# xbc and z of a hybrid encoder layer in one stated order, xbc by half slabs

## The chip, the core and the metric

The kernel runs on one core of a Trainium2 chip. The metric is the device time of one execution in microseconds. Three executions of the kernel before took 1104.84, 1105.65 and 1106.17 us (median 1105.65). The engines are named as in the profile: PE (TensorE), ACT (ScalarE), DVE (VectorE), POOL (GpSimd), SP (SyncE, which here only issues DMAs).

## The reference

One encoder layer on 256 tokens of width 2048, in float32. The part that matters here is the first of three blocks:

```python
hn = rmsnorm(h, mix_norm_pre[i])
proj = hn @ w_in[i]
z, xbc, dt_raw, u = jnp.split(proj, split_at, axis=-1)
y_ssd = ssd_mixer(z, xbc, dt_raw, ssd_conv_w[i], ssd_conv_b[i], ssd_dt_bias[i],
                  ssd_a_log[i], ssd_d[i], ssd_norm[i])
y_pool = pool_mixer(u, pool_w[i], pool_scale[i])
mix = jnp.concatenate([y_ssd, y_pool], axis=-1) @ w_out[i]
h = h + rmsnorm(mix, mix_norm_post[i])
```

and inside the mixer (`y` is a scan over the tokens in both directions, in chunks of 128):

```python
xbc = jax.nn.silu(dwconv_centred(xbc, conv_w, conv_b))
xs, bm, cm = jnp.split(xbc, [D_SSD, D_SSD + G * SSD_STATE], axis=-1)
...
y = y_fwd + y_bwd + xs.astype(F32) * d_skip.astype(F32).reshape(G, E)[:, :, None]
y = y.reshape(b, L, D_SSD) * jax.nn.silu(z.astype(F32))
y = y.reshape(b, L, G, D_SSD // G)
y = y * lax.rsqrt(jnp.mean(y * y, axis=-1, keepdims=True) + EPS)
```

z has 1024 columns, xbc 1536 (xs 1024, B 256, C 256). Behind this block come a gated MLP (up and down, width 5632) and a per-layer embedding, which the change does not touch.

## The kernel before

Every float32 product is made of three matmuls. Each operand is split into a high part (ACT's cast, L157, or `put`) and a low part (DVE's subtraction, L158), and high x high, high x low and low x high are summed in PSUM (`mm`, L90). `split` makes the two halves of one weight piece of 128 x 1024 in one of five weight buffers; the weights come over SP into one of three raw buffers. Names in the profile end in `w` for such a pair (`wo010_0w`: output projection, half 0, rows from 10 x 128, piece 0).

The stages follow one another on PE: dtu to 52 us, xbc 52 to 141, z 141 to 196, the output projection (`wo`, two halves of 1024 columns) 196 to 284, then up, down and the embedding.

**xbc** has three slabs of 512 columns, computed as columns x tokens: `feature_major` (L371) loads the weights of a slab in four pieces of two k-pairs and issues for each k and each 128 columns three matmuls of 256 tokens, summed in one PSUM tile. Behind each slab `times_rows` (L451), `conv` (L459, five taps: one on ACT, four on DVE), tanh on ACT and a last DVE product make the convolved, activated slab `cv`. Slab 2 holds B and C, slabs 0 and 1 hold xs.

**Jobs.** Between the pieces of xbc and z, `aside` (L220) pops a list of jobs from `work` and runs them: `pool_mix` (mx) and `pool_map` (pw) of the pooling mixer, `decays` (dps), `seg_sums` (cps, seg_x, seg_w), `seg` (eight segment-sum tiles, into E), `cb` (products of C and B), `weigh` (E times dt and cb), `xs_turn` (transposes, xt), `far`, `skip` and `mix` (four parts of y: matmuls yo and yd, additions on DVE). The jobs `early_fetch` and `early_add` prepare block sums of w_out for the units (0,0), (0,2), (1,0) and (1,2) of the output projection: fetch 1 MB, four additions of 512 columns in place (L275, `add_blocks`), store to DRAM over POOL's queue.

**z** (`token_major`, L330) is computed as tokens x columns in four PSUM tiles, z0_0 to z1_1. Behind it y is gated with silu(z) (tanh L812 on ACT, L813 and L814 on DVE), squared and summed (L815, ACT), the scale computed on POOL (L410 to L817), y scaled (L820, DVE) and transposed by PE (yt, L827) as the left operand of the projection. The projection begins with the rows of the pooling mixer (wo08 to wo014), which do not need y.

**Seven products.** Some units of the projection (wo00, wo02, wo112, wo10, wo12) are made with seven block products in place of eight (`seven_products`, L277): aw and bw are splits of the weights, dw and cw of their block sums. If the sums were prepared, they are loaded (tile `t`); otherwise DVE makes them in place between bw and dw.

**What sets the order.** A tile scheduler orders each engine's instructions, and assigns buffers, from the program's order and its own estimates. `in_order()` (L205) chains the instructions of ACT, DVE and SP that a block issues, so that they keep the order of the code; before, xbc and z are not in such a block. `load` issues DMAs on SP. PSUM has six main tiles and two misc tiles.

Of the kernel before, what the change touches and what calls it, by code (L numbers as in the profile page):

```python
# [17 lines left out]
P = 128  # L18
L = 256
# [34 lines left out]
def build(nc, a, out):  # L54
# [6 lines left out]
    with tile.TileContext(nc) as tc, \  # L61
# [208 lines left out]
        def add_blocks(r, t=None):  # L270
# [3 lines left out]
            for i, a, b in ((1, v, 0), (0, v, 3), (3, s, 1), (2, s, 3)):  # L274
                nc.vector.tensor_add(s[:, i], v[:, i], a[:, b])  # L275

# [94 lines left out]
        def feature_major(name, w, get, acc):  # L371

            for u in range(4):
                r = raw(f"{name}r{u}", w[u])
                for j in range(2):
                    wh, wl = split(f"{name}{u}_{j}", r[:, j * 1024:(j + 1) * 1024], 1024)
                    for kk in range(2):
                        k = 4 * u + 2 * j + kk
                        xh, xl = get(k)
                        for f in range(4):  # L380
                            s = slice(kk * 512 + f * P, kk * 512 + (f + 1) * P)
                            for q, (ww, xx) in enumerate(((wh, xh), (wh, xl), (wl, xh))):
                                mm(acc[f // 2][:, f % 2 * L:(f % 2 + 1) * L], ww[:, s], xx,
                                   k == 0 and q == 0 and f % 2 == 0, k == NK - 1 and q == 2)
                aside()

# [64 lines left out]
        def times_rows(name, acc, rb):  # L451
            o = mid(name)
            for i in range(2):
                nc.vector.tensor_tensor(o[:, i * 512:(i + 1) * 512].rearrange("p (f t) -> p f t", f=2),
                                        acc[i].rearrange("p (f t) -> p f t", f=2),
                                        rb.unsqueeze(1).to_broadcast([P, 2, L]), op=ALU.mult)
            return o

        def conv(name, acc, taps, wcol, wstep, bcol):  # L459

            cv = mid(name)
            half = taps // 2
            for f in range(4):
                o, i = cv[:, f * L:(f + 1) * L], acc[:, f * L:(f + 1) * L]
                nc.scalar.activation(o, i, AF.Identity, bias=vec(bcol + f), scale=vec(wcol + half * wstep + f))
                for j in range(taps):
                    d = j - half
                    if d == 0:
                        continue
                    lo, hi = max(0, -d), L - max(0, d)  # L470
                    nc.vector.scalar_tensor_tensor(o[:, lo:hi], i[:, lo + d:hi + d], vec(wcol + j * wstep + f),
                                                   o[:, lo:hi], op0=ALU.mult, op1=ALU.add)
            return cv


        hn = Panel("hn")
# [136 lines left out]
        ee = [page(f"E{t}") for t in range(2)]  # L613

        def seg_sums():

            cps = misc("cps")
            for a_ in range(4):
                mm(cps[:64, a_ * P:(a_ + 1) * P], da4[:, a_ // 2, a_ % 2].rearrange("p r h -> p (r h)"),
                   mask[:, 3 * (a_ % 2), :], True, True)  # L620
            hi, c = page("seg_h", F32R)[:64, :512], page("seg_c")[:64, :512]
            nc.scalar.copy(hi, cps[:64, :])
            nc.vector.scalar_tensor_tensor(c, hi.bitcast(F32), low, cps[:64, :], op0=ALU.mult, op1=ALU.add)
            c4 = c.rearrange("p (a l) -> p a l", a=4)
            for i in range(4):
                nc.scalar.activation(seg_x[:32, :, i, :], c4[:32], AF.Copy, scale=among[:32, i:i + 1])
            for i in range(4):
                nc.scalar.activation(seg_w[32:64, :, i, :], c4[32:], AF.Copy, scale=four[32:, i:i + 1])

        def seg(i):  # L630
            t, q = divmod(i, 4)
            ps = [misc(f"seg{i}{d}") for d in range(2)]
            for d in range(2):
                mm(ps[d], seg_w[:, 2 * t + d, q], seg_x[:, 2 * t + d].rearrange("p i l -> p (i l)"), True, True)
            e = ee[t][:, q * 512:(q + 1) * 512]
            nc.scalar.copy(e, ps[0])
            nc.vector.tensor_tensor(e, ps[1], e, op=ALU.min)
            nc.scalar.activation(e, e, AF.Exp)
# [3 lines left out]
        cat.hi, cat.lo = [None, page("cath1", F32R)], [None, page("catl1", F32R)]  # L642
        mixh, mixl = page("mixh", F32R), page("mixl", F32R)
        pw = {}

        def pool_mix(g):
            ps = misc(f"mx{g}")
# [706 lines left out]
```

## Time and profile before

| what | us |
|---|---|
| median of three runs | 1105.65 (1104.84 to 1106.17) |
| the profiled execution's own time | 1104.97 |
| its span | 1103.2 |
| PE busy | 1096.7 |
| DVE busy | 977.2 |
| ACT busy | 729.1 |
| xbc, first matmul | 52.24 |
| z, first matmul | 140.67 |
| output projection, first matmul | 196.31 |

The granted clock of PE was 0.999 over the span. Times of the trace count from the span's start. A row of the page's groups of instructions gives line, engine, operation, output and input, count, then busy time, mean ns of one, and the idle time before them with what ended it. A row of the timeline gives start, length, engine and line; in brackets stands how long the engine stood idle before it and who ended that. A row of the chain of waits gives start, length and what ran.

### The profile page before, as it was taken

The numbers are of one execution on the slowest core, as the hardware profiler recorded it, in microseconds if no ns is written. First come the engines' busy times: TensorE is split into PE (matmuls) and PEld (weight loads), VectorE is DVE, ScalarE is ACT, GpSimd is POOL, SyncE is SP. The second block draws the span as 40 slices with busy tenths as digits, with TensorE's granted clock in tenths as the row PEclk, the third lists the DMA queues.
The fourth block names the chain that finished last, engine by engine and source line by source line (L and its number), as shares of the span: only waits on it lengthen the run. The fifth ranks groups of instructions, "written<-read, shape, count | busy, mean of one in ns | idle before, by whom it ended". The sixth has DMA issues, their size and how long they took to land.

```text
span 1103.2 us, 16052 instructions
## 1 busy us (share of the span) xinstructions
PE 1096.7 (99%) x5961; PEld 948.8 (86%) x5961; DVE 977.2 (89%) x1373; ACT 729.1 (66%) x1068; POOL 84.9 (8%) x145
## 2 busy tenths in 40 slices
PE   9999999999999999999999999999999999999998
PEld 9999988888888888888888888888888888888886
DVE  6589998898868998889889988898999999999997
ACT  6858763566776565655656646657688878786773
POOL 0200000100100000000000000000000000051001
PEclk9999999999999999999999999999999999999999
DMA  9895259556489999989999998999999989996872
GB/s 363 359 339 195 101 183 367 209 195 244 158 367 388 408 397 364 403 344 367 383 366 383 364 391 345 404 362 420 367 410 375 378 335 389 419 379 224 317 276 77
DMA packets 57247, 361.71 MB, mean 328 GB/s; under 512 B 6352, under 2 KB 7504, under 8 KB 21200
## 3 DMA queue, kind: packets, MB, share of 16 engines
q1 hardware_dynamic: 45648, 298.71, 69.0%
q0 software_dynamic: 11088, 61.35, 14.5%
q8 instruction: 47, 0.77, 0.3%
q10 hardware_dynamic: 432, 0.62, 0.2%
q14 instruction: 32, 0.26, 0.1%
HBM read 306.65 MB, written 54.00 MB: 327 GB/s over the span
## 4 chain that ended last, share of the span: by engine, by line
PE 97%; ACT 1%; DVE 1%; issue 0%; POOL 0%; POOLq 0%; DVEq 0%
PE ga L90 22%; PE va L90 22%; PE dna L90 11%; PE woa L90 7%; PE xbc L90 5%; PE gt L90 5%; PE dns L90 4%; PE dtu L90 4%; PE z L90 4%; PE dn0s L90 2%; PE dn1s L90 2%; PE ple L90 1%; PE gts L90 1%; PE wos L90 1%; PE yd L90 1%; PE pw L90 1%
## 5 line engine op out<-in xcount | busy, mean ns | idle before, releaser
L90 PE MATMUL ga<-wox,ug_0w 128*128 128x512 f32 x704 | 130.8, 337 | 0.0
L90 PE MATMUL ga<-wox,ug_1w 128*128 128x512 f32 x704 | 130.2, 337 | 0.0
L90 PE MATMUL va<-wox,uv_0w 128*128 128x512 f32 x704 | 129.2, 337 | 0.0
L90 PE MATMUL va<-wox,uv_1w 128*128 128x512 f32 x704 | 129.2, 337 | 0.0
L90 PEld LDWEIGHTS ga<-wox,ug_0w 128*128 128x128 f32 x704 | 107.7, 188 | 14.6 <-ACT pl L919 0.2
L90 PEld LDWEIGHTS ga<-wox,ug_1w 128*128 128x128 f32 x704 | 107.5, 188 | 14.5 <-DVE wox L195 0.2
L90 PEld LDWEIGHTS va<-wox,uv_1w 128*128 128x128 f32 x704 | 107.5, 188 | 14.5
L90 PEld LDWEIGHTS va<-wox,uv_0w 128*128 128x128 f32 x704 | 107.5, 188 | 14.5
L275 DVE TENSOR_TENSOR dnb<-dnb 128x512 f32<-128x512 f32 x128 | 88.3, 690 | 3.0
L250 POOL DMA_DIRECT2D dns<-dnb x30 | 16.1, 536 | 319.4 <-DVE dnb L275 279.1
L90 PE MATMUL xbc<-hnh,xb_0w 128*128 128x256 f32 x192 | 37.9, 284 | 0.3 <-ACT u L571 0.3
L90 PE MATMUL xbc<-hnh,xb_1w 128*128 128x256 f32 x192 | 37.1, 283 | 0.0
L846 ACT CAST he<-he 128x512 fp32r<-128x512 f32 x13 | 8.1, 621 | 42.6 <-DVE he L845 42.6
L988 ACT CAST hs<-hid 128x384 fp32r<-128x384 f32 (+1 forms) x44 | 23.4, 537 | 13.7 <-PE dna L90 13.5
L90 PEld LDWEIGHTS xbc<-hnh,xb_0w 128*128 128x128 f32 x192 | 30.8, 189 | 0.9 <-ACT u L571 0.4
L90 PEld LDWEIGHTS xbc<-hnh,xb_1w 128*128 128x128 f32 x192 | 30.7, 189 | 0.1
L1068 ACT ACTIVATE fc<-gr,vt 128x256 f32<-128x256 f32 x44 | 26.1, 593 | 6.9 <-DVE gr L1061 6.9
L90 PE MATMUL dna<-dn_0w,hs 128*128 128x512 f32 x108 | 28.6, 394 | 0.0
L90 PE MATMUL dna<-dn_1w,hs 128*128 128x512 f32 x108 | 28.3, 392 | 0.0
L1139 POOL DMA_DIRECT2D hd<-hsum x24 | 12.9, 539 | 193.1 <-PE dn0s L90 70.4
L989 DVE TENSOR_TENSOR hs<-hid,hs 128x384 fp32r<-128x384 f32 (+1 forms) x44 | 25.4, 581 | 2.6 <-ACT hs L988 2.6
L90 PE MATMUL xbc<-hnl,xb_1w 128*128 128x256 f32 x96 | 27.3, 284 | 0.0
(1781 smaller groups left out, 2871.4 us busy)
## 6 DMA issues: line engine op xcount, KB each, us to landing
dnb<-w_down SPq DMA_DIRECT2D x32, 1024.0 KB, 10.0
dns<-dnb POOLq DMA_DIRECT2D x30, 1024.0 KB, 6.5
hd<-hsum POOLq DMA_DIRECT2D x24, 512.0 KB, 8.2
zr<-w_z SPq DMA_DIRECT2D x8, 1024.0 KB, 5.0
dtur<-w_dtu SPq DMA_DIRECT2D x14, 528.0 KB, 8.5
hsum<-he POOLq DMA_DIRECT2D x13, 512.0 KB, 7.7
wo0r<-w_out_ SPq DMA_DIRECT2D x6, 1024.0 KB, 6.2
gtb<-w_gate SPq DMA_DIRECT2D x6, 1024.0 KB, 9.6
```

What stands on the lines that cost most here:

```text
L90: last["pe"] = ins(nc.tensor.matmul(o, lhsT, rhs, start=start, stop=stop, skip_group_check=True))
L250: nc.gpsimd.dma_start(t, pg[0])
L275: nc.vector.tensor_add(s[:, i], v[:, i], a[:, b])
L846: nc.scalar.copy(o[:, :512], s[:, :512])
L988: nc.scalar.copy(t[:, :c1], hid_part(k)[:, :c1])
L989: nc.vector.tensor_sub(t[:, 512:512 + c1], hid_part(k)[:, :c1], t[:, :c1].bitcast(F32))
L1068: nc.scalar.activation(c[:, f], v[:, f], AF.Identity, bias=vec(V_FCB + 4 * s + 2 * i + f), scale=vec(w + NF))
L1139: nc.gpsimd.dma_start(o.bitcast(F32), kept[k])
```

## The change

1. The normalised input `hn` is kept as pairs, high and low side by side, and xbc is computed by half slabs of 256 columns (six, with four pieces each) by `feature_pairs`, as the stage up does: per k and 128 columns one matmul of 512 (high weight x both parts) and one of 256 (low weight x high part). The weights are laid out anew. `half_slab_out` brings a half slab out: ACT copies 2 x 256 from PSUM, DVE adds 2 x 256, and then as before, in phases.
2. xbc and z stand in one `in_order()` block, with jobs as generators: at each piece every running job does one phase (`go_on`), the next weight piece is split, and new jobs begin by the table `begin`, by piece (0 to 23 xbc, 24 to 31 z).
3. Jobs move: `pool_map` 1 to 3, `weigh(0, 1)`, `early_add(0, 2)` and the fetch of (1,0) begin later, `early_add(1, 0)` stands in the work of the projection. The pair (1, 2) is not prepared any more. Block (0,·) sums have a buffer of their own.
4. `seg` uses two main PSUM tiles, `mix` adds yd ahead of ym, and E, cat and mix pages are claimed when first used.

The diff, cut:

```diff
         def early_fetch(c, k):
-            early_raw[c, k] = page(f"wob{c}_{k}")
+            early_raw[c, k] = page(f"wob{c}_{k}") if c else ep.tile([P, 2048], F32, tag="wob", bufs=1, name=f"wob{c}_{k}")
             load(early_raw[c, k], w_out[c, k // 2])
 
         def early_add(c, k):
             r = early_raw.pop((c, k))
-            add_blocks(r)
+            yield from block_adds(r)
...
-        hn = Panel("hn")
+        hn = Pairs("hn")
...
         def seg(i):
             t, q = divmod(i, 4)
-            ps = [misc(f"seg{i}{d}") for d in range(2)]
+            if q == 0:
+                ee[t] = page(f"E{t}")
+            ps = main(f"seg{i}")
             for d in range(2):
                 mm(ps[d], seg_w[:, 2 * t + d, q], seg_x[:, 2 * t + d].rearrange("p i l -> p (i l)"), True, True)
+            yield
...
-        def xbc(slab):
-            acc = main(f"xbc{slab}")
-            feature_major(f"xb{slab}", w_xbc[slab], hn, acc)
...
+        def half_slab_out(slab, i, acc):
+
+            if i == 0:
+                conved[slab] = mid(f"cv{slab}")
+            sc = ep.tile([P, 512], F32, tag="xr", bufs=2, name=f"xr{slab}{i}")
+            out = conved[slab][:, i * 512:(i + 1) * 512]
+            w0 = V_SCW + 4 * slab + 2 * i
+            for f in range(2):
+                nc.scalar.copy(sc[:, f * L:(f + 1) * L], acc[f][:, L:])
+            yield
+            for f in range(2):
+                s = slice(f * L, (f + 1) * L)
+                nc.vector.tensor_add(sc[:, s], sc[:, s], acc[f][:, :L])
+            v = sc.rearrange("p (f t) -> p f t", f=2)
+            nc.vector.tensor_tensor(v, v, rxb.unsqueeze(1).to_broadcast([P, 2, L]), op=ALU.mult)
+            yield
...
+            nc.scalar.activation(sc, out, AF.Tanh, scale=0.5)
+            yield
+            nc.vector.scalar_tensor_tensor(out, sc, 1.0, out, op0=ALU.add, op1=ALU.mult)
...
-        work[4].append(job(early_fetch, 1, 2))
-        work[6].append(job(early_add, 1, 2))
-        zacc = [main(f"z{t}") for t in range(2)]
-        token_major("z", w_z, 0, list(range(NK)), hn, zacc)
+        begin = {
+            1: [lambda: pool_mix(0)], 2: [lambda: pool_mix(1)], 4: [lambda: pool_mix(2)], 5: [lambda: pool_mix(3)],
+            6: [seg_sums], 7: [decays], 9: [lambda: early_fetch(0, 0)],
...
+            28: [lambda: skip(0), lambda: skip(1), lambda: mix(0, 0)], 29: [lambda: mix(0, 1), lambda: early_add(0, 2)],
+            30: [lambda: mix(1, 0)], 31: [lambda: mix(1, 1), lambda: early_fetch(1, 0)],
+        }
...
+        def z_step(n):
+            go_on()
+            next_piece()
+            go_on()
+            next_piece()
+            start(n)
+
+        zacc = []
+        with in_order():
+            for _ in range(5):
+                next_piece()
+            for n in range(24):
+                slab, i, q = (2, 0, 1)[n // 8], n // 4 % 2, n % 4
+                if q == 0:
+                    acc = main(f"xbc{slab}{i}")
+                feature_pairs(q, ready.pop(f"xb{slab}{i}{q // 2}_{q % 2}"), hn, acc)
...
+            work.extend([lambda n=n: z_step(n)] for n in range(24, 32))
+            zacc.extend(main(f"z{t}") for t in range(2))
+            token_major("z", w_z, 0, list(range(NK)), hn, zacc)
+            while going:
+                go_on()
...
-        work.extend([[], [job(y_turn, 0)], [job(y_turn, 2), job(y_turn, 4)], [job(y_turn, 6)]])
+        work.extend([[lambda: list(early_add(1, 0))], [job(y_turn, 0)], [job(y_turn, 2), job(y_turn, 4)], [job(y_turn, 6)]])
...
-        "w_xbc": tiles(w_in[:, DSSD:c_dt], 4, 512),
+        "w_xbc": tiles(w_in[:, DSSD:c_dt], 8, 256),
```

The gating, scaling and transposing lines of before (L812 to L827) have the numbers L855 to L873 in the changed kernel, `mix` has L762 to L765.

Three places in the order of the engines. The first is DVE in the last part of z; before, twelve rows in a row, from the low split of the first half of wo010 on:

```order
L158 TENSOR_TENSOR wo010_0w_2147<-wo0r10_2145,wo010_0w_2147 128x1024
L741 TENSOR_TENSOR y_1671<-y_1671,ym01_1973 128x512
L739 TENSOR_TENSOR ym10_1988<-yo10_1986,dec_624 128x512
L746 TENSOR_TENSOR y_1671<-y_1671,yd01_1976 128x512
L741 TENSOR_TENSOR y_1671<-y_1671,ym10_1988 128x512
L813 SCALAR_TENSOR_TENSOR zt_2054<-zt_2054,z0_0_1672 128x512
L746 TENSOR_TENSOR y_1671<-y_1671,yd10_1991 128x512
L814 TENSOR_TENSOR y_1671<-y_1671,zt_2054 128x512
L813 SCALAR_TENSOR_TENSOR zt_2054<-zt_2054,z0_1_1673 128x512
L814 TENSOR_TENSOR y_1671<-y_1671,zt_2054 128x512
L158 TENSOR_TENSOR wo010_1w_2150<-wo0r10_2145,wo010_1w_2150 128x1024
L739 TENSOR_TENSOR ym11_2041<-yo11_2039,dec_624 128x512
```

and in the changed kernel, twelve rows that end with the same split:

```order
L275 TENSOR_TENSOR wob1_0_1878<-wob1_0_1878 128x512
L762 TENSOR_TENSOR ym11_1880<-yo11_1867,dec_624 128x512
L764 TENSOR_TENSOR y_627<-y_627,yd11_1869 128x512
L857 TENSOR_TENSOR y_627<-y_627,zt_1884 128x512
L765 TENSOR_TENSOR y_627<-y_627,ym11_1880 128x512
L275 TENSOR_TENSOR wob1_0_1878<-wob1_0_1878 128x512
L863 TENSOR_SCALAR y_627<-y_627,yn0r_1901 128x512 x2
L856 SCALAR_TENSOR_TENSOR zt_1884<-zt_1884,z1_0_1453 128x512
L856 SCALAR_TENSOR_TENSOR zt_1884<-zt_1884,z1_1_1454 128x512
L857 TENSOR_TENSOR y_627<-y_627,zt_1884 128x512 x2
L275 TENSOR_TENSOR wob1_0_1878<-wob1_0_1878 128x512
L158 TENSOR_TENSOR wo010_0w_1983<-wo0r10_1981,wo010_0w_1983 128x1024
```

Before, wo010_0w is split ahead of all gating, both halves of y0 (L814) are gated ahead of anything that reads yd11 or yo11, and the addition of yd11 stands four rows behind the last one shown. Now the second half of y0 is gated (L857) behind the addition of yd11 (L764), and wo010_0w is split behind the scaling of y0 (L863), the gating of y1 and two block additions of wob1_0.

The second is SP in the output projection (r: weights, t: prepared block sums), before:

```order
L120 DMA wo00r_2288<-w_out_ 128x1536
L120 DMA wo02r_2333<-w_out_ 128x1536
L120 DMA wo0r4_2370<-w_out_ 128x2048
L120 DMA wo00t_2290<-wos0_0_864 128x2048
L120 DMA wo02t_2335<-wos0_2_926 128x2048
L120 DMA wo0r6_2413<-w_out_ 128x2048
L120 DMA wo1r8_2468<-w_out_ 128x2048
```

and now:

```order
L120 DMA wo0r14_2072<-w_out_ 128x2048
L120 DMA wo00r_2124<-w_out_ 128x1536
L120 DMA wo02r_2169<-w_out_ 128x1536
L120 DMA wo0r4_2206<-w_out_ 128x2048
L120 DMA wo0r6_2249<-w_out_ 128x2048
L120 DMA wo00t_2126<-wos0_0_1359 128x2048
L120 DMA wo02t_2171<-wos0_2_1826 128x2048
```

The loads of wo00t and wo02t have gone behind that of wo0r6; those of h0 and h1 have moved ahead of wo0r14.

The third is DVE in the second half of the projection, at the unit wo12, before:

```order
L158 TENSOR_TENSOR wo12aw_2623<-wo12r_2619,wo12aw_2623 128x512
L158 TENSOR_TENSOR wo12bw_2626<-wo12r_2619,wo12bw_2626 128x1024
L158 TENSOR_TENSOR wo12dw_2629<-wo12t_2621,wo12dw_2629 128x1024
L158 TENSOR_TENSOR wo12cw_2632<-wo12t_2621,wo12cw_2632 128x1024
L158 TENSOR_TENSOR wo114_0w_2658<-wo1r14_2656,wo114_0w_2658 128x1024
```

and now:

```order
L158 TENSOR_TENSOR wo12aw_2457<-wo12r_2455,wo12aw_2457 128x512
L158 TENSOR_TENSOR wo12bw_2460<-wo12r_2455,wo12bw_2460 128x1024
L275 TENSOR_TENSOR wo12r_2455<-wo12r_2455 128x512 x4
L158 TENSOR_TENSOR wo12dw_2467<-wo12r_2455,wo12dw_2467 128x1024
L158 TENSOR_TENSOR wo12cw_2470<-wo12r_2455,wo12cw_2470 128x1024
```

The block sums, which came from DRAM as wo12t, are now made in place by four additions between the splits wo12bw and wo12dw.

More of the change, by code (lines that the diff above doesn't have):

```diff
@@ L369, in token_major @@
                 at[nu]()
[L371 to L385, printed above, removed]
         def feature_pairs(n, part, get, acc):
@@ L687, in cb, with xs_turn @@
                 nc.scalar.activation(cbm[:, 2, g, s, :], og, AF.Copy, scale=0.25)
-        def xs_turn(cv, slab):
+        def xs_turn(slab):
+            cv, pss = conved[slab], []
             for t in range(2):
                 ps = misc(f"xt{slab}{t}")
+                pss.append(ps)
                 for f in range(4):
                     nc.tensor.transpose(ps[:, f * P:(f + 1) * P], cv[:, f * L + t * P:f * L + (t + 1) * P], ident)
+            yield
+            for t, ps in enumerate(pss):
@@ new lines, in build, with go_on, start @@
+        going = []
+        def go_on():
+            for g in list(going):
+                if next(g, g) is g:
+                    going.remove(g)
+        def start(n):
+            for f in begin.pop(n, ()):
+                g = f()
+                if hasattr(g, "__next__") and next(g, g) is not g:
+                    going.append(g)
+        pieces = [(f"xb{s}{i}{u}", w_xbc[2 * s + i, u], j) for s in (2, 0, 1) for i in range(2) for u in range(2) for j in range(2)]
+        pieces += [(f"z{2 * u}", w_z[0, u], j) for u in range(NK // 2) for j in range(2)]
@@ new lines, in build, with next_piece @@
+        fetched = {}
+        def next_piece():
+            if not pieces:
+                return
+            name, src, j = pieces.pop(0)
+            if j == 0:
+                fetched["raw"] = raw(f"{name}r", src)
+            ready[f"{name}_{j}"] = split(f"{name}_{j}", fetched["raw"][:, j * 1024:(j + 1) * 1024], 1024)
+        def z_step(n):
[13 more added lines that the diff above has]
+                feature_pairs(q, ready.pop(f"xb{slab}{i}{q // 2}_{q % 2}"), hn, acc)
+                if q == 3:
+                    done = half_slab_out(slab, i, acc)
+                    next(done)
+                    go_on()
+                    next(done)
+                    next_piece()
+                    next(done)
+                    going.append(done)
+                else:
+                    go_on()
+                    next_piece()
+                start(n)
+            work.extend([lambda n=n: z_step(n)] for n in range(24, 32))
+            zacc.extend(main(f"z{t}") for t in range(2))
+            token_major("z", w_z, 0, list(range(NK)), hn, zacc)
+            while going:
+                go_on()
@@ L800, in build @@
+        assert not (work or pieces or begin or ready)
         zt = page("zt")
```

151 lines of the change are left out of this document (69 added, 82 removed).

## The prediction

> **What bounds the kernel now.** First the page: who is busy, and what the chain of waits is made of.
>
> ```profile
> PE 1096.7 (99%) x5961; PEld 948.8 (86%) x5961; DVE 977.2 (89%) x1373; ACT 729.1 (66%) x1068; POOL 84.9 (8%) x145
> PE 97%; ACT 1%; DVE 1%; issue 0%; POOL 0%; POOLq 0%; DVEq 0%
> ```
>
> PE is busy for 99% of the span and makes 97% of the chain. A time can fall only where PE gets less to do or where one of its waits goes, and any new wait of PE moves everything behind it. So I looked for PE's waits in the stages that change (the waits view, 52 to 200 us), and at the load of each engine there (the stretches view: PE, PEld, DVE, ACT, POOL busy; xbc is 52 to 141, z 141 to 197, the last two are parts of the output projection).
>
> ```profile
> PE xbc L90 <- ACT u L571: 0.3, 1, 0.3
> PE seg L90 <- ACT E L636: 0.2, 1, 0.2
> ...
> 52.00:141.00 89.00, 88.56 (x707) 86.20 (x708) 83.12 (x155) 61.70 (x106) 3.15 (x5) 1.00 0.57 208
> 141.00:197.00 56.00, 56.00 (x275) 45.81 (x274) 49.21 (x76) 28.89 (x47) 2.46 (x6) 1.00 0.66 255
> 197.00:220.00 23.00, 23.00 (x110) 18.85 (x109) 20.20 (x35) 12.86 (x22) 2.87 (x5) 1.00 0.62 247
> 252.00:284.00 32.00, 32.00 (x139) 25.84 (x138) 27.20 (x30) 20.10 (x26) 1.81 (x6) 1.00 0.63 230
> ```
>
> PE waits 0.5 us in the whole of xbc and z and nothing behind. There is next to nothing to win from waits: 0.5 us. But DVE is at 83 of 89 us and 49 of 56, so an order that puts a needed DVE instruction late has little slack to hide in. That is where I looked for losses.
>
> **Term 1, the form of the xbc matmuls.** Pieces of the chain of waits (start, length, what), of xbc before and of the stage up, which already has the new form:
>
> ```profile
> 128.36 5.71 PE xbc L90 x48
> ...
> 315.85 22.19 PE va L90 x128
> ...
> 140.67 22.09 PE z L90 x96
> ```
>
> Now three matmuls of 256 columns stand for each weight tile: 5.71 / 48 = 119 ns each, 357 ns for three. After, one of 512 and one of 256: 22.19 / 64 pairs = 347 ns. There are 576 / 3 = 192 triples, so 192 x 10.3 ns = **2.0 us less**. Put together from z's 512 columns (22.09 / 96 = 230 ns) and the 119, a pair is 349 ns and the gain 1.5 us; I take 2.0, since up's row is the new form itself. [...]
>
> **Term 2, DVE and ACT in xbc.** Twelve additions of 256 columns come in on DVE and twelve copies on ACT; eight block additions, one weighing and most of three pool maps leave xbc for z. Prices by the groups of instructions:
>
> ```profile
> L403 DVE TENSOR_TENSOR gr<-gr,ga 128x256 f32<-128x256 f32 x44 | 16.4, 413 | 0.2 <-ACT gr L402 0.2
> L275 DVE TENSOR_TENSOR wob<-wob 128x512 f32<-128x512 f32 x12 | 8.2, 686 | 0.1
> L714 DVE SCALAR_TENSOR_TENSOR w<-cbm,dt,w 128x128 f32<-128x128 f32 x16 | 4.5, 341 | 0.0
> ```
>
> In: 12 x 0.413 = 5.0 us. Out: 8 x 0.686 = 5.5 us, and 8 x 0.341 = 2.7 us of weighing besides. So DVE's load in xbc falls by some 3 us, to about 80 of 87. The old waits (0.5 us) may go and new ones come, because all DVE work now stands in one stated order and a wait at its head holds the rest. PE reuses six PSUM buffers that DVE and ACT must empty, and the segment sums now take two of them each. The lower end is nothing: in xbc before DVE was at 93% and PE waited 0.5 us. The upper end is 3.8 us: if DVE were busy throughout from 80 us on, the 28 - 24.66 = 3.3 us that it stands idle in the first stretch could not be made good, and 0.5 us stays.
>
> ```profile
> 52.00:80.00 28.00, 27.76 (x230) 27.29 (x231) 24.66 (x49) 14.88 (x22) 2.62 (x4) 1.00 0.81 303
> ```
>
> I take 0.5 us, near the row of the whole stage. With the old 0.5 us gone that is **0**.
>
> **Term 3, from z into the output projection.** What leaves xbc lands in z, where DVE has 56 - 49.2 = 6.8 us free; block additions of (1,0) (4 x 0.69), the weighing (2.7 and a product) and pool maps take all of that. More important is the order at the end. Timeline rows of DVE, ACT and POOL before (start, length, engine, line):
>
> ```profile
> 184.38 1.22 DVE L158 TENSOR_TENSOR wo_0w<-wo0r,wo_0w 128x1024 fp32r<-128x1024 f32 x1
> 192.43 0.69 DVE L814 TENSOR_TENSOR y<-y,zt 128x512 f32<-128x512 f32 x1
> 194.08 0.63 ACT L815 ACTIVATE zt<-y 128x512 f32<-128x512 f32 x1
> 196.90 0.49 DVE L820 TENSOR_SCALAR y<-y,yn0r 128x512 f32<-128x512 f32 x1 [0.87 <-POOL yn0r L817]
> 198.90 1.28 DVE L813 SCALAR_TENSOR_TENSOR zt<-zt,z 128x512 f32<-128x512 f32 x2
> 200.09 1.29 DVE L814 TENSOR_TENSOR y<-y,zt 128x512 f32<-128x512 f32 x2
> 201.30 1.22 DVE L158 TENSOR_TENSOR wo_0w<-wo0r,wo_0w 128x1024 fp32r<-128x1024 f32 x1
> 201.44 0.62 ACT L815 ACTIVATE zt<-y 128x512 f32<-128x512 f32 x1
> 205.03 0.88 DVE L820 TENSOR_SCALAR y<-y,yn1r 128x512 f32<-128x512 f32 x2 [1.38 <-POOL yn1r L817]
> ...
> 194.58 1.73 PE yd L90 x16
> 196.31 11.10 PE woa L90 x48
> ...
> 213.40 0.87 PE yt L827 x8
> ```
>
> PE leaves z with yd11, at 196.31. The second weight pair of the projection, wo010_0w, was split by DVE at 184.38, twelve microseconds early. In the new order of DVE (below the diff) it stands behind the whole end of y. That end now hangs on PE: gating the second half of y0 stands behind the addition of yd11, which waits for PE's last matmul of z. From there, counted from z's end: addition 0.7, gating to 1.4, square on ACT, then scaling. Square to scaling was 194.08 to 196.90 = 2.8 us and 201.44 to 205.03 = 3.6 us, so DVE scales y0 at 4.3 to 5.0. Behind that in the queue: two scalings 0.8, gating of y1 1.2 + 1.2 (198.90 to 200.09 to 201.30), a block addition 0.6, the split 1.2: done at 9.3 to 10.0. PE has two weight pairs before it (11.10 / 48 x 24 = 5.55 us), the high half of wo010_0w (4 x 0.23 = 0.9) and two transposes (0.87 / 8 x 2 = 0.2): it needs the low half at 6.7. So PE waits 2.6 to 3.3 us where it waited for nothing. Below, 0 if DVE is ahead by other means. I take **2.6 us more**. It goes to the end of the kernel, since the up and dn stages behind are PE's.
>
> **Term 4, the block sums wo00t.** SP's queue, the landing time (issues view: KB each, us), and who used it:
>
> ```profile
> 208.64 0.37 SPq L120 DMA_DIRECT2D wo00t<-wos  x1
> 213.20 0.33 SPq L120 DMA_DIRECT2D wo0r<-w_out_  x1
> ...
> wo00t<-wos SPq DMA_DIRECT2D x1, 1024.0 KB, 8.1
> wo00r<-w_out_ SPq DMA_DIRECT2D x1, 768.0 KB, 4.1
> ...
> 211.96 1.22 DVE L158 TENSOR_TENSOR wo00bw<-wo00r,wo00bw 128x1024 fp32r<-128x1024 f32 x1
> 217.94 1.23 DVE L158 TENSOR_TENSOR wo00dw<-wo00t,wo00dw 128x1024 fp32r<-128x1024 f32 x1
> 221.49 0.63 PE L90 MATMUL woa<-wo00dw,cath 128*128 128x512 f32 x2
> ```
>
> The load of wo0r6 (213.20) waits for the split of wo00bw (211.96 + 1.2), which frees its buffer. wo00t and wo02t stood ahead of it on SP and now stand behind it. Both sides of this step move with term 3 alike, so I count in the old times: wo00t leaves at 213.20 + 0.43 = 213.6, five microseconds later. It landed after 8.1 us, at 216.74, and DVE was through with its low half at 217.94 + 1.2 = 219.1, 2.4 us behind. With 8.1 us again that is 213.6 + 8.1 + 2.4 = 224.1; PE needs it at 221.49 + 0.23 = 221.7: a wait of 2.4 us. If it lands as fast for its size as wo00r did (4.1 x 4 / 3 = 5.5 us), none. I take **1.5 us more**, nearer to its own row.
>
> **Term 5, the unit wo12.** The block sums of (1,2) were made in z and loaded; now DVE makes them in place, between the splits wo12bw and wo12dw. The unit wo112 before did the same, and gives the price:
>
> ```profile
> 248.69 1.41 DVE L275 TENSOR_TENSOR wo112r<-wo112r 128x512 f32<-128x512 f32 x2
> 250.19 1.05 ACT L157 CAST wo112dw<-wo112r 128x1024 fp32r<-128x1024 f32 x1 [2.69 <-DVE wo112r L275]
> 251.27 1.22 DVE L158 TENSOR_TENSOR wo112dw<-wo112r,wo112dw 128x1024 fp32r<-128x1024 f32 x1 [1.17 <-ACT wo112dw L157]
> ...
> 259.17 1.22 DVE L158 TENSOR_TENSOR wo12bw<-wo12r,wo12bw 128x1024 fp32r<-128x1024 f32 x1
> 261.14 1.23 DVE L158 TENSOR_TENSOR wo12dw<-wo12t,wo12dw 128x1024 fp32r<-128x1024 f32 x1 [0.76 <-ACT wo12dw L157]
> 263.36 0.63 PE L90 MATMUL woa<-wo12dw,cath 128*128 128x512 f32 x2
> ```
>
> Two additions take 1.4 us, four 2.8. From the last addition's end (250.10) to the end of the low half (251.27 + 1.22 = 252.49) were 2.4 us: ACT's cast, then DVE. For wo12: 259.17 + 1.2 + 2.8 + 2.4 = 265.6, and PE needs it at 263.36 + 0.23 = 263.6: a wait of 2.0. When the sums were loaded the lead was 263.6 - (261.14 + 1.2) = 1.3 us; five weight buffers set it, and they do not change. If ACT's cast (1.05) could run beside the last addition, the wait would be 1.0; no row shows that. I take **1.6 us more**.
>
> **Sum.** -2.0 + 0 + 2.6 + 1.5 + 1.6 = +3.7 us. The span of the profiled execution was 1103.2 us and its time 1104.97 us, 1.77 us around the span, which the change leaves alone. 1104.97 + 3.7 = **1108.7 us**. The median of the three runs was 1105.65, 0.7 above the profiled one. A measurement of this kernel tells 0.2% from no change, 2.2 us: "same" is 1103.4 to 1107.9.
>
> **Rivals.**
>
> DVE is ahead at the end of z (not slower). If the stated order lets DVE reach the split wo010_0w within 6.7 us of z's end, term 3 is nothing, and with DVE early wo00bw is split early too, so that term 4 goes with it: 1104.97 - 2.0 + 1.6 = 1104.6 us. It decides at 2.6 us of lead. For it: DVE's load in xbc falls by 3 us, and nothing but PE's last matmul holds y back. Against: the measured 2.8 us from square to scaling cannot be moved ahead of yd11 in this order. If the wait at wo12 is hidden also, and the 0.5 us of old waits go, 1102.5 us; only this is faster.
>
> DVE becomes the bound in xbc (slower still). Term 2 at its upper end: 1108.7 + 3.8 = 1112.5 us. For it: buffers of six for xbc, z and now the segment sums, and the 3.3 us of early idle. Against: DVE's lighter load there. It decides if DVE has no idle left between 80 and 135 us.
>
> The new form saves nothing, because two matmuls of 256 columns cost no more than one of 512 once jobs of other shapes stand between. Then 1108.7 + 2.0 = 1110.7 us. For it: up's pairs run 128 in a row, xbc's will not. Against: z's 512 columns take 230 ns, and two of xbc's 256 take 238, in stages that both have jobs. [...]
>
> **How the numbers follow.** The forecast has 0.50 (1106 to 1111: 0.20 of it in "same", 0.30 slower); DVE ahead 0.27 (0.15 faster, 0.12 same); DVE as the bound 0.13, all slower; the form without gain 0.10 (0.04 same, where terms 4 or 5 also fall short, 0.06 slower). That gives faster 0.15, same 0.36, slower 0.49. The range runs from 1102.8, which leaves out about half of the faster cases, to 1112.5, which leaves out the upper half of the bound case.
>
> **What will show it.** Term 1: pieces of xbc with 32 matmuls in 5.5 us. Term 2: xbc's waits for E or xr (DVE), and z's start near 139 us. Term 3: PE waiting for wo010_0w's low half (L158, named wo_0w) for 2.6 us about 6 us behind yd11, and DVE there behind a wait for yn0r. Term 4: ACT's cast of wo00dw waiting for the DMA of wo00t, and PE for it. Term 5: four additions before wo12dw and a wait of PE for it. I am wrong if PE waits nowhere in the projection, or if its waits in xbc and z pass 4 us.

## The result, and the profile after

The changed kernel takes 1116.75 us (median of four, 1116.3 to 1117.7), the one before 1105.53: a ratio of 1.0103, 95% interval 1.0085 to 1.012. It is slower by 11.2 us; forecast was 1108.7 with a range from 1102.8 to 1112.5. The profiled execution took 1117.7 us with a span of 1115.9. Some executions of the kernel before and of two variants below (e13, e14) take 5 to 6 us more, and e13's profile, which caught one, shows no wait of PE for it, so kernels that ran once are compared by stages.

First the page of the changed kernel: busy time, and the slices of PE and of its granted clock.

```profile
PE 1101.1 (99%) x5769; PEld 941.4 (84%) x5769; DVE 984.9 (88%) x1388; ACT 730.4 (65%) x1083; POOL 83.0 (7%) x144
PE   9999899999999999999999999999999999999998
PEclk9999899999999999999999999999999999999999
```

PE is still busy for 99%. The fifth slice (112 to 140 us) falls under 9 in both rows, in the busy share and in the granted clock. The waits view of PE says for whom:

```profile
PE seg L90 <- DVE E L608: 4.0, 1, 4.0
PE woa L90 <- DVE wo_0w L158: 2.3, 1, 2.3
PE woa L90 <- ACT wo12dw L157: 0.9, 1, 0.9
PE woa L90 <- ACT wo00dw L157: 0.4, 1, 0.4
PE seg L90 <- ACT E L606: 0.3, 1, 0.3
PE wos L90 <- ACT wo12cw L157: 0.2, 1, 0.2
PE wos L90 <- ACT wo00cw L157: 0.2, 1, 0.2
```

Three of the places are those of the prediction (wo010_0w, wo12, wo00). The largest is not: a segment sum waits 4.0 us for E in xbc. With the 0.3 us of the next one, that passes the 4 us at which the prediction called itself wrong. The stretches view around the two long waits (us, PE busy, PEld, DVE, ACT, POOL, then the granted clock):

```profile
116.00:120.00 4.00, 3.54 (x20) 2.82 (x18) 3.89 (x9) 3.03 (x5) 0.00 (x0) 1.00 0.00 0
120.00:126.00 6.00, 2.12 (x4) 1.21 (x5) 5.51 (x9) 3.03 (x6) 0.00 (x0) 0.77 0.49 175
126.00:132.00 6.00, 6.00 (x28) 5.29 (x27) 5.93 (x10) 4.05 (x9) 0.00 (x0) 0.66 0.52 178
202.00:212.00 10.00, 7.68 (x35) 6.04 (x34) 8.52 (x14) 5.10 (x10) 4.09 (x8) 1.00 0.10 41
212.00:224.00 12.00, 12.00 (x53) 9.74 (x52) 9.86 (x16) 4.54 (x8) 3.35 (x3) 0.86 0.81 277
```

Each wait is followed by a stretch in which PE's clock is lower: 0.66 of full from 126 to 132 us, with PE busy throughout, and 0.86 from 212 to 224. These are means of a full and a half clock: it was 0.50 from 123.29 to 130.12 us and from 212.04 to 215.45, where matmuls of 512 columns start 427 ns apart, and 1.00 between the two, where they start 231 ns apart.

So the loss can be added up from the matmul records, as the time by which their starts lie further apart than at full rate: at the segment sums 4.2 + 0.9 us of waiting and 2.7 us of half clock; at wo010_0w 2.5 us and 1.6 of half clock; at wo00 1.2; at wo12 1.6. That is 14.7 us. By stages (first matmul of xbc to the first of the projection; from there to the first of the stage up; from there to the last matmul; all by the starts of the matmul records, which put the projection before at 196.12 us, where the row of the chain has 196.31):

| kernel | xbc and z | projection to up | up to the last matmul |
|---|---|---|---|
| before | 143.9 | 93.9 | 807.9 |
| changed | 149.1 | 100.4 | 808.6 |

xbc and z lose 5.2 us (7.8 us of losses, so 2.6 must have been gained), the projection 6.5. What stands behind is unchanged within 0.7 us.

**Why DVE was late.** The row of E that PE waits for is DVE's, at 122.80. The timelines of ACT and DVE in the changed kernel, from 30 us ahead of it, show what it stood behind.

```profile
98.39 0.57 ACT L606 COPY E<-seg 128x512 f32<-128x512 f32 x1
103.19 0.28 ACT L675 ACTIVATE cbm<-cb 128x128 f32<-128x128 f32 x1 [4.22 <-issue]
104.02 0.28 ACT L675 ACTIVATE cbm<-cb 128x128 f32<-128x128 f32 x1 [0.55 <-DVE cbm L673]
104.19 1.04 ACT L157 CAST xb_0w<-xb101r 128x1024 fp32r<-128x1024 f32 x1
...
92.72 1.23 DVE L158 TENSOR_TENSOR xb_1w<-xb011r,xb_1w 128x1024 fp32r<-128x1024 f32 x1 [2.47 <-ACT xb_1w L157]
102.63 0.48 DVE L673 SCALAR_TENSOR_TENSOR cbm<-cb,small 128x128 f32<-128x128 f32 x2
103.50 0.49 DVE L673 SCALAR_TENSOR_TENSOR cbm<-cb,small 128x128 f32<-128x128 f32 x2 [0.39 <-ACT cbm L675]
105.27 1.22 DVE L158 TENSOR_TENSOR xb_0w<-xb101r,xb_0w 128x1024 fp32r<-128x1024 f32 x1 [1.28 <-ACT xb_0w L157]
107.89 0.49 DVE L673 SCALAR_TENSOR_TENSOR cbm<-cb,small 128x128 f32<-128x128 f32 x2 [0.40 <-ACT cbm L675]
109.66 1.22 DVE L158 TENSOR_TENSOR xb_1w<-xb101r,xb_1w 128x1024 fp32r<-128x1024 f32 x1 [1.28 <-ACT xb_1w L157]
122.80 0.69 DVE L608 TENSOR_TENSOR E<-seg,E 128x512 f32<-128x512 f32 x1
```

The job cb writes in turns: two DVE products, one ACT copy, two DVE products, one ACT copy, out of one PSUM tile. In the stated order all of it is one phase on both engines. ACT stands 4.2 us at the head of its queue; the row names no releaser, but the copy starts 0.08 us after DVE's first two products end. The weight cast xb101_0w stands behind the second turn, and DVE, through with its own part, waits 1.28 us for that cast. With the second cb the same again: 0.39 + 1.28 + 0.40 + 1.28 = 3.35 us of DVE lost. From 109.66 to 122.80 DVE has no gap, so it does not catch up before PE needs E. Another wait of DVE (2.47 us ahead of 92.72, for a cast behind the four seg_w scalings) was nearly as large. Was it one, the other, or both, or the PSUM tiles that the segment sums now take from xbc?

### The profile page after: what moved, and what is told of

The parts are those of the page before. It is cut to its first block, busy times and chain, and to the rows that moved or that the text cites. A ratio compares the mean times of both kernels' runs of the same rounds, so it can differ in the third digit from the quotient of the medians.

```text
span 1115.9 us, 15688 instructions
## 1 busy us (share of the span) xinstructions
PE 1101.1 (99%) x5769; PEld 941.4 (84%) x5769; DVE 984.9 (88%) x1388; ACT 730.4 (65%) x1083; POOL 83.0 (7%) x144
## 4 chain that ended last, share of the span: by engine, by line
PE 92%; DVE 5%; ACT 1%; issue 1%; DMA 1%; POOL 0%; POOLq 0%; DVEq 0%; ACTq 0%
PE ga L90 22%; PE va L90 22%; PE dna L90 11%; PE gt L90 5%; PE dns L90 4%; PE dtu L90 4%; PE woa L90 4%; PE z L90 4%; PE xbc L90 4%; PE dn0s L90 2%; PE dn1s L90 2%; PE ple L90 1%; PE gts L90 1%; DMA wo1r<-w_out_ 1%; DVE cv L714 1%
## 5 line engine op out<-in xcount | busy, mean ns | idle before, releaser
L90 PE MATMUL xbc<-hn,xb_0w 128*128 128x512 f32 x192 | 38.3, 351 | 0.0
L90 PE MATMUL xbc<-hn,xb_1w 128*128 128x512 f32 (+1 forms) x192 | 37.5, 343 | 0.0
L90 PEld LDWEIGHTS xbc<-hn,xb_0w 128*128 128x128 f32 x192 | 30.8, 196 | 4.9 <-DVE E L608 0.3
L90 PEld LDWEIGHTS xbc<-hn,xb_1w 128*128 128x128 f32 x192 | 30.1, 190 | 4.2 <-issue 0.2
L90 PE MATMUL woa<-wo_0w,cath 128*128 128x512 f32 x88 | 26.3, 401 | 2.3 <-DVE wo_0w L158 2.3
L1185 POOL DMA_DIRECT2D hd<-hsum x24 | 12.7, 529 | 193.0 <-PE dn0s L90 84.8
```

The costliest lines, as they stand in the source:

```text
L90: last["pe"] = ins(nc.tensor.matmul(o, lhsT, rhs, start=start, stop=stop, skip_group_check=True))
L1185: nc.gpsimd.dma_start(o.bitcast(F32), kept[k])
```

## The experiments

Theory A: waits between ACT and DVE in the stated order make DVE late. Rival B: the segment sums' move to the main PSUM tiles. Rival C: DVE has too much work in xbc in any order. All edits are to the changed kernel unless said otherwise.

**e1, no stated order.**

```diff
-        with in_order():
+        with nullcontext():
```

> The changed kernel with xbc and z outside the stated order (the scheduler orders ACT, DVE and SP there), all else kept: half slabs, jobs in phases, table. Theory A (in the stated order ACT and DVE wait for each other, 5.8 us of DVE's idle time between 88 and 110 us, so DVE empties the segment-sum tiles late): the 4.2 us wait of PE at 119 us and the half clock behind it go, z begins near 133.5 us instead of 141.2, about 1109 us. Rival B (PSUM: the segment sums take main tiles) and rival C (DVE has too much work in xbc whatever the order): PE still waits 3 us or more there, 1114 us or more.

Measured: 1103.32 us, the kernel before beside it 1105.03. That is 5.7 us less than theory A had, because the waits of the projection went as well. xbc and z take 140.9 us, the projection 94.9. PE's waits in the waits view:

```profile
PE woa L90 <- ACT wo12dw L157: 0.2, 1, 0.2
PE wos L90 <- ACT wo12cw L157: 0.2, 1, 0.2
```

and the stretch of xbc:

```profile
52.00:134.00 82.00, 82.00 (x488) 72.11 (x488) 78.94 (x149) 61.52 (x106) 2.53 (x3) 1.00 0.56 206
```

The changed kernel, for comparison:

```profile
52.00:141.00 89.00, 84.46 (x477) 72.88 (x476) 79.17 (x146) 58.94 (x103) 1.35 (x3) 0.96 0.46 166
```

The same instructions, with DVE busier (78.94 of 82 us, against 79.17 of 89 in the changed kernel), and PE does not wait once in xbc. That speaks against C, and against B taken alone: the tiles are the same. The stated order loses 8.1 us in xbc and z and 5.6 in the projection.

**e2, cb in phases.**

```diff
             for s in range(2):
                 dg = ps[:, s * L + s * P:s * L + (s + 1) * P]
...
+            yield
+            for s in range(2):
+                og = ps[:, s * L + (1 - s) * P:s * L + (2 - s) * P]
                 nc.scalar.activation(cbm[:, 2, g, s, :], og, AF.Copy, scale=0.25)
```

> Only the job cb is cut finer: its four DVE products in one phase, its two ACT copies in the next, so that they no longer take turns. A: 3.3 us of DVE's idle time (0.39 + 1.28 + 0.40 + 1.28) go, PE's wait at 119 us falls from 4.2 to about 1 us and the half clock behind it goes too, about 1110.5 us. B and C: the wait stays within 1 us of 4.2, 1116 us.

Measured: 1110.39 us. The waits view, and the stretch in which the changed kernel had its long wait:

```profile
PE woa L90 <- ACT wo00dw L157: 2.0, 1, 2.0
PE woa L90 <- DVE wo_1w L158: 1.0, 1, 1.0
PE woa L90 <- ACT wo12dw L157: 0.9, 1, 0.9
PE seg L90 <- DVE E L608: 0.6, 1, 0.6
PE seg L90 <- ACT E L606: 0.6, 1, 0.6
...
118.00:124.00 6.00, 4.64 (x23) 3.35 (x22) 5.58 (x8) 4.93 (x9) 0.00 (x0) 1.00 0.41 156
```

The wait for E falls from 4.0 to 0.6 us and the clock stays at 1.00. xbc and z take 143.2 us, 5.8 less. A is right about this stage. That the total fits its number to 0.1 us is in part luck, since the projection changed too: the scheduler, which orders what stands outside the block, now lets DVE gate the second half of y0 ahead of the addition of yd11, and the wait for wo010_0w shrinks to one of 1.0 us for wo010_1w. Without the longer wait ahead of it, wo00dw now waits 2.0 us: there term 4 stands bare, and the cast names its cause:

```profile
216.42 0.42 SPq L120 DMA_DIRECT2D wo00t<-wos  x1
...
224.34 1.04 ACT L157 CAST wo00dw<-wo00t 128x1024 fp32r<-128x1024 f32 x1 [1.48 <-DMA wo00t<-wos]
```

**e3, the scalings spread; e4, both.**

```diff
                 nc.scalar.activation(seg_x[:32, :, i, :], c4[:32], AF.Copy, scale=among[:32, i:i + 1])
-            yield
+                if i % 2:
+                    yield
...
                 nc.scalar.activation(seg_w[32:64, :, i, :], c4[32:], AF.Copy, scale=four[32:, i:i + 1])
+                if i == 1:
+                    yield
```

> Only the eight scalings seg_x and seg_w of the segment sums are spread over four phases of two instead of two of four, so that a weight cast stands behind two of them and not four. A: 2.5 us of DVE's idle time go, PE's wait at 119 us falls to about 2 us, 1111 to 1114 us by whether the clock halves behind it. B and C: unchanged, 1116 us.

> Both cuts together. A: all 5.8 us of DVE's idle time go, PE does not wait at 119 us and keeps its full clock, z begins near 133.5 us, 1109 us. B: the wait stays near 4 us. C: a wait of over 2 us stays, since DVE's work in xbc is the same.

Measured: 1118.33 and 1110.85 us. Alone the edit leaves a wait of 3.2 us for E, and xbc and z take 148.9 us; with cb in phases they take 143.5 against 143.2 without. The times that A gave are missed in both. But the edit did not do what it was meant to do. DVE's waits for casts in e3 at this place:

```profile
90.26 1.22 DVE L158 TENSOR_TENSOR xb_1w<-xb011r,xb_1w 128x1024 fp32r<-128x1024 f32 x1 [0.56 <-ACT xb_1w L157]
94.64 1.23 DVE L158 TENSOR_TENSOR xb_0w<-xb100r,xb_0w 128x1024 fp32r<-128x1024 f32 x1 [1.16 <-ACT xb_0w L157]
98.69 1.23 DVE L158 TENSOR_TENSOR xb_1w<-xb100r,xb_1w 128x1024 fp32r<-128x1024 f32 x1 [0.87 <-ACT xb_1w L157]
```

They come to 2.6 us, as much as the one wait of 2.47 us that they replace, and in e4 they are the same within 0.02 us. So these runs do not show what the waits behind seg_w cost PE. The waits at cb are shown to cost it (e2). The 2.3 us by which xbc and z of e2 are still longer than those of e1 are not explained.

**e5, segment sums back in the misc tiles.**

```diff
-            ps = main(f"seg{i}")
+            ps = [misc(f"seg{i}{d}") for d in range(2)]
```

> Only the segment sums go back to the two misc tiles of PSUM, the six main tiles are left to xbc and z. B: PE's wait of 4.2 us at 119 us goes with the half clock, 1109 us. A and C: DVE is as late as before, PE waits 3 us or more for a tile somewhere between 110 and 130 us, 1114 us or more.

Measured: 1123.23 us, slower than the changed kernel. Neither side had all of it. The 4 us wait at 119 us goes, and xbc and z take 141.4 us, as B said. But the projection takes 114.4 us:

```profile
PE woa L90 <- DVE wo_0w L158: 4.0, 1, 4.0
PE woa L90 <- ACT wo00dw L157: 3.5, 1, 3.5
PE yt L873 <- DVE y L863: 1.4, 1, 1.4
```

PE ran ahead through z and met DVE's delay at the end of y. So the main tiles decide where PE meets DVE's delay. They do not make it: DVE loses the same 3.35 us at cb, and 2.6 us more there in two waits for PE's products of C and B. From xbc to up e5 takes 255.7 us, 6.2 more than the changed kernel. The long wait in xbc needs both the stated order and the main tiles, since e1 and e5 each take it away; only e1 also takes away the loss.

**e6, wo08 and wo010 split in the stated order, ahead of y's end.**

```diff
+        pieces += [(f"wo0{k}", w_out[0, k // 2], j) for k in (8, 10) for j in range(2)]
         fetched = {}
...
```

> Only the splits of wo08 and wo010 are taken into the stated order behind the last pieces of z, ahead of the end of y. Theory: the wait of 2.5 us for wo010_0w and the 1.6 us of slower matmuls behind it (its own consequence) go, 4.1 us less, 1112.6 us. Rival: y's end is late by itself, and PE waits as long for the transposes of y or for wo012: 1115 us or more. Second question: if the clock drop is not due to the wait, 1.6 us stay and it ends at 1114.2.

Measured: 1114.85 us. The wait for wo010_0w is gone, and so is the clock drop behind it (the mean granted clock of the span is 0.996, in the changed kernel 0.994); a wait of 1.7 us for the transposes of y (`PE yt L874 <- DVE y L864`) has come. From xbc to up it is 2.4 us shorter than the changed kernel, 1.7 less than hoped for. Both halves of the expectation hold in part: the clock drop went with the wait, and y's end is late by itself.

**e7, wo00t ahead of wo0r6 on SP; e8, the sums of (1,2) prepared again.**

```diff
-        IN_ORDER = ('dn1',)
+        IN_ORDER = ('dn1', 'wo00', 'wo02', 'wo0r4', 'wo0r6')
```

```diff
-        work.extend([[lambda: list(early_add(1, 0))], ..., [job(y_turn, 6)]])
+        work.extend([[lambda: list(early_add(1, 0)), job(early_fetch, 1, 2)], ..., [job(y_turn, 6), lambda: list(early_add(1, 2))]])
```

> Only the loads of wo00 to wo06 keep the order of the code on SP, so that wo00t and wo02t stand ahead of wo0r6 again. Theory: the waits of PE for wo00dw and wo00cw (1.2 us together) go, 1115.5 us. Rival: the load is late for another reason (it leaves late with DVE), at most 0.5 us go, 1116.3 us.

> Only the block sums of (1,2) are prepared again, in the first half of the output projection, and loaded. Theory: the waits for wo12dw and wo12cw (1.6 us together) go, 1115.1 us. Rival: the four additions only move and delay a split of the first half by as much, 1116.7 us.

Measured: 1116.01 and 1113.48 us. In e7 no wait is left at wo00, but the projection is only 0.1 us shorter: of the 1.2 us gained, 0.5 are lost again between wo02 and wo112, and 0.5 at wo12, where wo12dw waits 1.4 us instead of 0.9. In e8 no wait is left at wo12, and none over 0.3 us at wo00; the projection takes 98.4 us, 2.1 less. So both waits have the causes that the prediction gave them, but removing the first gains next to nothing. Of e8's time 0.9 us come from xbc, where the slow matmuls end earlier: the chain's row of 11 matmuls takes 1.97 us from 128.18 on, in the changed kernel 2.71 us from 128.62 on.

**e9, e13, e14: what is left without the stated order.** e9 is e1 with e8's edit, e13 is e1 again, e14 has the fetch four and the additions three entries of the job list later than e9 (the fetch leaves at 205.7 us instead of 184.3, the first addition starts at 220.2 instead of 203.9):

```diff
+                     [job(early_fetch, 1, 2)], [], [lambda: list(early_add(1, 2))]])
```

> The changed kernel without the stated order (as e1_free_order), and with the block sums of (1,2) prepared again in the first half of the projection (as e8_sums12_back). Theory: what is left of e1's waits, 1.0 us at wo12, goes too; the form of the matmuls is then all that remains of the change, 2.0 us better than before plus the 0.5 us of old waits: 0.2% faster than before, about 1102.5 us beside 1105. Rival: the four additions delay something else, no better than e1's 1103.3.

> The kernel of e1_free_order once more, timed in rounds against the kernel before. If e1's single look (1103.3 beside 1105.0) holds, the ratio is 0.998 to 0.999 and the change without its stated order is the faster kernel by some 2 us; if that look was luck, the ratio is 1.000 within its interval.

> As e13, and the block sums of (1,2) prepared late in the first half of the projection, so that their load and their four additions stand behind the load of wo00t (in e9 they stood ahead of it, and PE waited 1.9 us for wo00dw). Theory: PE waits neither at wo00 nor at wo12, 1.0 us less than e13, about 1102.3 us. Rival: the additions delay a split of wo04 to wo110, no gain over e13.

The profiled executions, from which the last two columns come, took 1106.95 us (e9), 1108.89 (e13) and 1102.05 (e14).

| kernel | median us | ratio to before | xbc and z | projection |
|---|---|---|---|---|
| e9 | 1103.97 | 0.9985 (0.9973 to 0.9997) | 140.8 | 97.7 |
| e13 | 1104.55 | 0.9985 (0.9964 to 1.0006) | 140.8 | 94.6 |
| e14 | 1103.05 | 0.9979 (0.9958 to 1.0001) | 140.8 | 93.7 |

e9 does no better than e1, as its rival said: the four additions stand ahead of the load of wo00t and PE waits 1.7 us for wo00dw, with the clock at 0.72 from 220 to 226 us. In e13 the ratio is as forecast, but its interval holds 1. In e14 the waits view of PE has one line, from the start of the kernel:

```profile
PE dtu L109 <- POOL ident masks.py:199: 1.4, 1, 1.4
```

From xbc to up e14 takes 234.5 us, 3.3 less than before. That is the best version here, 0.2% faster by the median; its interval just reaches 1, and only e9's stays below it. So the change without its stated order is at most a little faster than before, and how much of that is the form and how much the moved jobs is not shown: no run has the jobs moved without the form.

**e10, e11: can the stated order be mended?** e10 has the edits of e2, e7 and e8; e11 that of e6 besides.

> The changed kernel with the stated order and three mends: cb in phases (as e2), the loads of wo00 to wo06 in the code's order on SP (as e7), the sums of (1,2) prepared again (as e8). Theory: e2's 1110.4 us less its waits at wo00 (2.2 + 0.6 us) and wo12 (1.05 + 0.6 us): 1106 us, within 0.2% of before; PE keeps its full clock throughout. Rival: waits move on to the next place, 1108 us or more.

> As e10_mended_order, and the splits of wo08 and wo010 in the stated order ahead of y's end (as e6). Theory: 1.5 us of waits at wo010 go and up to 1.9 us at the transposes of y come: within 1 us of e10.

Measured: 1113.67 us (ratio 1.0081, 1.0066 to 1.0097) and 1114.70. The forecast of 1106 falls, its rival holds; e11 lies 1.0 us above e10, the edge of what was expected. In e10 wo00dw waits 1.8 us though its load has left early: DVE splits wo00bw at 220.01, behind the four additions that e8's edit brings, the cast on ACT stands behind two more steps of y, and slow matmuls follow (two of 512 columns take 0.85 us from 228.43 on). With DVE late at y's end, each thing that is put right there delays the next.

**e12, the form alone.** The kernel before, with the pairs, half slabs and twelve additions, and jobs, places and the free order as they were.

```diff
-            feature_major(f"xb{slab}", w_xbc[slab], hn, acc)
-            sc = times_rows(f"xr{slab}", acc, rxb)
...
+                        feature_pairs(2 * u + j, split(f"xb{slab}{i}{u}_{j}", r[:, j * 1024:(j + 1) * 1024], 1024), hn, acc)
...
+                total(o, acc)
```

> The kernel before with the form of xbc alone: hn as pairs, half slabs, 16 matmuls of 512 and 16 of 256 columns for each half slab and piece group, ACT's copies and DVE's additions; jobs, their places and the scheduler's order as before. Theory: 192 pairs save 10 ns each, 2.0 us; DVE has room for twelve additions: 1103 us, z begins near 138.7 us. Rival: without the moved jobs DVE (93% busy in xbc before, 5 us more now) becomes the bound there, z begins after 140 us, 1105 us or more.

Measured: 1109.35 us, ratio 1.0036 (1.0022 to 1.0049). PE is through with xbc at 138.7 us, where the theory had z begin. Then the rival's loss comes: DVE is busy for 85.83 of 89 us, has ten products of the convolution (140.82 to 144.85) ahead of the split of z_1w, and PE waits for that at the start of z.

```profile
PE z L90 <- DVE z_1w L158: 3.5, 1, 3.5
...
52.00:141.00 89.00, 88.42 (x523) 77.01 (x524) 85.83 (x167) 66.15 (x119) 2.87 (x5) 1.00 0.55 201
142.00:146.00 4.00, 0.50 (x3) 0.07 (x1) 4.00 (x10) 1.92 (x3) 0.00 (x0) 0.99 0.00 0
146.00:152.00 6.00, 5.96 (x19) 4.81 (x20) 6.00 (x7) 4.00 (x10) 0.00 (x0) 0.72 0.81 261
```

So the twelve additions seem to need the room that the moved jobs make. That is argued from DVE's load and from the place of the wait: e12 differs from e1 also in the PSUM tiles of the segment sums and in the order that the scheduler finds. The gain does not need the stated order.

## Why the prediction was wrong

**Term 1 (2.0 us gained): right.** A stretch of xbc in the changed kernel:

```profile
81.14 11.20 PE xbc L90 x64
```

32 pairs in 11.20 us are 350 ns against 357 for three, 1.3 us in all, nearer to the 1.5 us that was put together from z's row than to up's. Over the whole stage it is more. Counted from each matmul's start to the next one's, xbc's matmuls take 70.6 us before and 68.5 in e1, in which PE waits nowhere in xbc and z: 2.1 us less, of which 0.3 is the old wait at the segment sums. xbc and z of e1 are 3.0 us shorter than before: the 2.1, 0.4 in the segment sums' own matmuls (4.2 to 3.7 us), and some 0.4 us in small pieces. The other old wait, 0.3 us, stands ahead of xbc's first matmul and is no part of this.

**Term 2 (0): this is the step that failed.** I took the waits in xbc as 0.5 us, because DVE's load there falls and because before PE waited 0.5 us with DVE at 93%. Load was the wrong measure. In the changed kernel DVE is less busy in xbc than before (79.2 of 89 us, against 83.1), and PE lost 7.8 us there, in place of the 0.5 us of the term. What counts in a stated order is whose head waits for whose; cb's turns between DVE and ACT, which the change left as they were, were harmless while the scheduler could put other work between them (in e1 DVE waits 0.2 us there and PE nowhere). Once it couldn't, they cost DVE 3.35 us in four waits, and cutting them into phases takes 5.8 us off the stage (e2). I had seen that the order holds what is behind a waiting head, and bounded it by 3.8 us from DVE's early idle time. The bound left out that ACT and DVE can wait for each other, and the clock. The rival "DVE becomes the bound in xbc" named the place, but by load, and at 1112.5 us.

**The clock: left out everywhere.** 4.3 us of the loss (2.7 of them among term 2's 7.8) are matmuls at half rate behind two waits. No row of the kernel before shows it: PE's longest wait there was 1.4 us and its granted clock 0.999 over the span. The bounds counted a wait at its own length.

**Term 3 (2.6): right.** PE waited 2.3 us by the waits view, 2.5 by the records' spacing, at the place and for the split that were named. The steps, in DVE's timeline of the changed kernel:

```profile
201.80 0.69 DVE L764 TENSOR_TENSOR y<-y,yd 128x512 f32<-128x512 f32 x1 [1.04 <-PE yd L90]
205.76 0.88 DVE L863 TENSOR_SCALAR y<-y,yn0r 128x512 f32<-128x512 f32 x2 [1.48 <-POOL yn0r L860]
209.56 1.22 DVE L158 TENSOR_TENSOR wo_0w<-wo0r,wo_0w 128x1024 fp32r<-128x1024 f32 x1
```

z ends at 201.8; scaling at 4.0 us behind it (forecast 4.3 to 5.0), the split done at 9.0 (9.3 to 10.0). The 1.6 us of half clock came on top.

**Term 4 (1.5): near in size, its road partly other.** 1.2 us here, and none at wo00 once the loads are put back (e7). But in the changed kernel the 2.5 us wait of term 3 had given the load time to land, and the cast of wo00dw came late on ACT's own queue; in e2, with only 1.1 us of waiting ahead, the late load costs 2.8 us by the records' spacing. That the sum came near 1.5 is luck.

**Term 5 (1.6): right.** 1.6 us by the records' spacing; DVE's four additions took 2.86 us and the low half began 1.16 us behind its cast:

```profile
271.46 2.86 DVE L275 TENSOR_TENSOR wo12r<-wo12r 128x512 f32<-128x512 f32 x4
275.49 1.23 DVE L158 TENSOR_TENSOR wo12dw<-wo12r,wo12dw 128x1024 fp32r<-128x1024 f32 x1 [1.16 <-ACT wo12dw L157]
```

**The sum.** Forecast +3.7 us. Terms 3 to 5 came to 5.3 us of waiting, forecast 5.7. With term 2's 7.8 us, 1.6 us of half clock behind term 3's wait and the 2.6 us gained, that is +12.1 us; the spans of the two profiled executions differ by 12.7 us, the medians by 11.2. The rival in which DVE is ahead at the end of z fell with the wait for wo010_0w; e1 shows that it describes the change without its stated order.

## What to carry to other kernels

Before work is put in a stated order on several engines, look for jobs in which two engines take turns within one step: here the scheduler put other work between the turns (e1), while in the stated order everything behind both heads waited, and DVE's busy share showed nothing of it. Price a PE wait with the half clock that may follow (here 2.7 us behind a wait of 4.0, 1.6 behind one of 2.3), and ask where a late engine's debt is paid next: here removing one wait uncovered, moved or lengthened another six times (e2, e5, e6, e7, e9, e10). A gain in matmuls that brings work to a nearly full engine (twelve additions here) can be lost there unless work is taken off it first, as e12 against e1 suggests.

## What the runs showed of the hardware

In the changed kernel PE ran at half clock behind its two long waits, of 4.0 and 2.3 us. By the stretches view its granted clock was 0.50 from 123.29 to 130.12 us and from 212.04 to 215.45, and 1.00 between the two. PE went on at 123.54 and at 210.84 us, so the first drop came 0.25 us before that and the second 1.2 us after. By the records' spacing 14 matmuls behind the first wait and 8 behind the second ran at half rate, 427 or 213 ns apart for 512 or 256 columns; at full clock those of xbc are 231 and 117 ns apart.

In other runs, by the waits view, and by the chain of waits, the stretches view or the record of the clock:

| run | PE's wait, us | what came behind it |
|---|---|---|
| e3, e6, e7, e8 | 3.2, 4.1, 4.1, 4.0 for E | 8 matmuls of xbc in 2.66, 2.73, 2.73, 2.70 us; 8 in 1.41 us in e1, which has no such wait |
| e12 | 3.5 for z_1w | granted clock 0.72 from 146 to 152 us |
| e3, e5 | 2.8, 3.5 for wo00dw | 2 matmuls of 512 columns in 0.85 us in each |
| e7, e8 | 2.3 for wo010_0w | 20 matmuls in 6.45 and 6.47 us; the next 24 in 5.54 and 5.55 |
| e11 | 2.1 for the transposes of y | 13 matmuls in 4.58 us; 24 later ones in 5.54 |
| e2 | 2.0 for wo00dw | granted clock 1.00 from 218 to 232 us |
| e4 | 1.8 for wo00dw | granted clock 1.000 over the span |
| e10 | 1.8 for wo00dw | 2 matmuls of 512 columns in 0.85 us |
| e6 | 1.7 for the transposes of y | 31 matmuls in 7.19 us, 232 ns each |
| e9 | 1.7 for wo00dw | granted clock 0.72 from 220 to 226 us |

Of the five waits from 1.7 to 2.0 us in the table two were followed by slow matmuls (e9, e10) and three were not (e2, e4, e6), so here the length alone does not sort them. What decides is not shown.
